# Up projection on the normalised x1 for three of its four quarters, first-norm sums in float32r, and another order in the last norm's tail

## Chip, core and metric

The kernel runs on one core of one Trainium2 chip. The metric is device time in microseconds (us). The kernel before takes 2334.99 us, the median of 3 runs (2334.02 to 2336.24). All matrix work is in 32-bit floats, most of it as float32r pairs.

## Reference

One layer of a hybrid decoder for 320 token columns (256 of a prompt, 8 x 8 of samples). Cut to what the change touches:

```python
merged = sigmoid(gate_a) * ya + sigmoid(gate_b) * yb
mix = merged @ w_out
x1  = LayerNorm(ALPHA * x + mix, ln1_g, ln1_b)          # ALPHA = 2 ** 0.25, D = 2048
hid = square(relu(x1 @ w_up))                           # 2048 -> 8192
ff  = hid @ w_down                                      # 8192 -> 2048
y   = LayerNorm(ALPHA * x1 + ff, ln2_g, ln2_b)
```

Before that stand one input projection, two recurrences (mLSTM and HGRN2) and two branch projections; the change leaves them as they are. The end states of the prompt, Cp and Sp, are outputs too, and are computed at the very end.

## The kernel before, in words

Activations lie transposed: 16 blocks of 128 channels (j or k, 0 to 15) by 320 token columns. A **tile** of the main stream is 128 output channels: 16 steps k, each of three matmuls in float32r, since weight and activation are each split in a rounded high part and a remainder: hi x hi, hi x lo, lo x hi (48 matmuls, accumulated in one bank of PSUM). The three are `self.mm(o, hi, mh)`, `self.mm(o, hi, ml)`, `self.mm(o, lo, mh)` in `run_main`; in the profile all matmuls have line L336. The tiles come in phases of 16: `wo` (w_out), then four quarters f = 0 to 3, each `up` (w_up) and `dn` (w_down). A phase is 768 matmuls. `moving(t)` says which activations a phase streams and which event each k waits for.

Weights arrive in units of 128 x 1024 (half a tile). `prep` splits each: ScalarE (ACT, L330, out `wh` or `bb`) writes the high part, VectorE (DVE, L475, out `wl` or `bb`) the remainder. Three buffers `wh`/`wl` serve from the start; at the start of `wo` the five wide buffers `wx` (in the memory `bb`) join them, so that eight units can be in flight. A unit's buffer is free again when PE has used it.

Everything else (evacuation of banks, the norms, the outputs) is written as generators that hand instructions to a list scheduler, `Sched`. It runs while the program is written: it keeps a clock per engine with fixed cost estimates and decides where in each engine's queue an instruction goes. On the chip every engine works through its queue in that order and waits by semaphores.

The first norm: `ev_wo` (L1790) makes z = ALPHA x + mix (L1797, L1801). After four tiles the sum S1 of z is added up over the channels by a matmul with a matrix of ones (`ln_add`, L1713), and the result c is taken off every z, so that later sums are small. S1 and S2 (sums of z and z squared, L1743, L1744) run on to j = 14; `ln_pre` multiplies them with ones and `ln_final` (L1754) adds the last z and its square by two more such matmuls: five in all, each in full float32. Then come mean M and 1/sigma RS by ACT and DVE (L1770 to L1778).

`up` doesn't wait for the norm: `zg` (L1814, L1819 in DVE's rows) splits z times gain into `xh`/`xl`, and two more columns there (320 and 321) carry the gain and the bias, so `up` streams 322 columns and `ev_up` (L1835) corrects the product with M and RS: `misc` from the two columns, L1840, L1842, ReLU, square, split into `ra`/`rxb` for `dn`. `x1` (L1822) makes ALPHA x1 for the residual, and `ev_dn` (L1852) adds each quarter of `dn` to it (L1857). In the last quarter the second norm's sums run along. **The tail** follows the last matmul of `dn`: ones matmuls, M and T (ACT), X (L1770, L1773, DVE), Ln and Exp (ACT), RS (L1776 to L1778, DVE), then per block subtract M (L1874) and multiply RS (L1879) on DVE in `y`, gain and bias on ACT and a DMA in `yb_`. Beside it `m_C` multiplies Cp (eight banks, copied out by ACT, `oC`) and `h_S` multiplies Sp (`oS`, four copies by ACT, four by DVE, L1557); SP issues all output DMAs in its queue's order.

Of the kernel before, what the change touches and what calls it, by code (L numbers as in the profile page):

```python
# [293 lines left out]
class Program:  # L294
# [251 lines left out]
    def moving(self, t):  # L546
        kind = t[0]
        if kind == "wa":
            return self.bah, self.bal, self.ba_ev
        if kind == "wb":  # L550
            return self.bbh, self.bbl, self.bb_ev
        if kind == "wo":
            return self.bah, self.bal, self.mg_ev
        if kind == "up":
            return self.xh2, self.xl2, self.zg_ev
        if kind == "dn":
            return self.bah, self.bal, self.hid_ev[t[2]]
        return self.xh, self.xl, None

    def before(self, i, t):  # L560
# [26 lines left out]
        elif kind == "wo" and h == 0:  # L587
# [3 lines left out]
            self.hl_free += [(s.t["pe"], x) for x in self.wx]  # L591
            s.spawn(self.ln_x(), 1)
        elif kind == "dn" and c == 3 and h == 0:
            self.carve_x()
        elif i == len(TILES) - 8:
            for j in range(MH):
                s.spawn(self.m_C(j), 3)
            for j in range(HH):
                s.spawn(self.h_S(j), 3)
# [477 lines left out]
    def m_C(self, h):  # L1077
# [7 lines left out]
        for c in range(2):  # L1085
# [8 lines left out]
            yield ("act", act(512, True), lambda: self.A(self.oC[h][:, c, :], b))  # L1094
# [603 lines left out]
    def ln_add(self, n, j, z, pre):  # L1698
# [4 lines left out]
        if j < 4:  # L1703
# [7 lines left out]
            if j == 3:  # L1711
                p = yield acq(self.sbank)
                yield ("pe", pe_f(TOK), lambda: self.mm(p[:, :TOK], self.ones, S1, start=True, stop=True))  # L1713
# [12 lines left out]
        if j == 15:  # L1726
            yield from self.ln_final(n, z)
            return
        yield from self.ln_sum(j, z)
        yield post(st["s"][j])  # L1730
        if j == 14:
            self.s.spawn(self.ln_pre(n), 0)

# [20 lines left out]
    def ln_final(self, n, z):  # L1754

        v = self.nc.vector
        st = self.ln[n]
        M, RS, X, T = (self.lnb[i] for i in (3, 4, 5, 6))
# [7 lines left out]
        yield post(st["fin"])  # L1766
        t = yield ("act", act(TOK, True), lambda: self.A(M, p1, scale=1.0 / D))
# [22 lines left out]
    def ev_wo(self, j, c, b):  # L1790
# [16 lines left out]
        if j == 15:  # L1807
            yield wait(*self.zg_ev)
            gb = self.vec[:, V_G1:V_G1 + 32]
            yield ("act", act(32), lambda: self.A(gb, gb, scale=ALPHA))  # L1810
# [21 lines left out]

    def ev_up(self, j, f, b):
        v = self.nc.vector

        sm = yield acq(self.sm)
# [13 lines left out]
    def ev_dn(self, j, f, b):  # L1850
# [6 lines left out]
        yield ("dve", dve(TOK, True), lambda: v.tensor_tensor(z, z, b[:, :TOK], ALU.add))  # L1857
# [8 lines left out]
    def y(self):  # L1866
# [4 lines left out]
        for i in range(KT + 2):  # L1871
# [3 lines left out]
            if i == 1:  # L1875
                yield wait(st["end"])
            if i > 1:
                z = self.acc[:, i - 2, :]
                t = yield ("dve", dve(TOK), lambda: v.tensor_tensor(z, z, self.lnb[4], ALU.mult), (0.0,))  # L1879
                self.s.spawn(self.yb_(i - 2, z), 0, t)  # L1880
# [9 lines left out]
    def run(self, pool):  # L1890
# [14 lines left out]
        self.acc_ev = [Ev() for _ in range(KT)]  # L1905
# [79 lines left out]
```

## Time and profile before

| | |
|---|---|
| median of 3 runs | 2334.99 us |
| the profiled execution's own time | 2335.47 us |
| its span, first to last instruction | 2333.5 us |
| PE busy | 2320.9 us (99%) |
| DVE busy, ACT busy | 1359.4 us (58%), 1074.2 us (46%) |
| granted TensorE clock | 0.998 |
| first matmul of `up` f = 0, f = 1, f = 2 | 1397.78, 1625.55, 1852.25 us |
| last matmul phase ends, first matmul of Cp | 2307.26 us |

Times inside the execution are us from the span's start. Matmuls overlap in a pipeline: one lasts some 310 ns in the record, but the next starts about 147 ns after it, so the distance between starts is what a matmul costs. A row of the timeline has start, duration, engine, line, operation, out<-in, shape and count, and in brackets how long the engine had been idle and what ended that; a row with x2 covers two instructions of one group. A float32 matmul (the ones) is recorded as x2.

### The profile page before, as it was taken

How to read it: one execution, taken by the hardware profiler on the slowest of the kernel's cores; microseconds unless marked ns; L12 is line 12 of the kernel's file. 1: busy time of each engine (PE TensorE's matmuls, PEld its weight loads, DVE VectorE, ACT ScalarE, POOL GpSimd, SP SyncE). 2: the span in 40 equal slices, each digit the busy share in tenths (PEclk: the TensorE clock that was granted, in tenths of full speed). 3: DMA queues.
4: the chain of work that ended last, by engine and by line, in shares of the span. 5: the costliest groups of instructions: out<-in, count | busy, mean ns of one | idle time of the engine just before them, and what ended most of it. 6: DMA issues, size and time to landing. Idle time of an engine off the chain costs nothing.

```text
span 2333.5 us, 38987 instructions
## 1 busy us (share of the span) xinstructions
PE 2320.9 (99%) x15812; PEld 2276.1 (98%) x15812; DVE 1359.4 (58%) x2304; ACT 1074.2 (46%) x1765; POOL 11.5 (0%) x36
## 2 busy tenths in 40 slices
PE   9999999999999999999999999999999999999998
PEld 8999999999999999999999999999999999999998
DVE  5565566667676776555555767544554455445555
ACT  4444445455566665444433546533443344334434
POOL 0000000000000000000000000000000000000000
PEclk9999999999999999999999999999999999999999
DMA  7576857665555555555555644444444444444465
GB/s 238 202 251 207 292 186 275 227 215 173 196 179 189 182 187 168 182 168 178 170 174 172 222 162 145 146 152 148 150 145 154 145 151 147 154 145 149 150 226 181
DMA packets 145627, 424.92 MB, mean 182 GB/s; under 512 B 18468, under 2 KB 39972, under 8 KB 144424
## 3 DMA queue, kind: packets, MB, share of 16 engines
q1 hardware_dynamic: 143864, 415.63, 53.6%
q0 software_dynamic: 1152, 6.29, 0.8%
q8 instruction: 123, 2.02, 0.3%
q10 hardware_dynamic: 432, 0.52, 0.1%
q14 instruction: 56, 0.46, 0.1%
HBM read 371.48 MB, written 50.90 MB: 181 GB/s over the span
## 4 chain that ended last, share of the span: by engine, by line
PE 97%; DMA 1%; DVE 1%; ACT 0%; issue 0%; SPq 0%; DVEq 0%; ACTq 0%
PE bank L336 95%; DMA wr<-wt 1%; DMA f<-xT 0%; DVE f3m L1874 0%; DVE f3m L1879 0%; PE bank L925 0%; PE bank L1586 0%; DMA gaD<-f 0%; PE bank L1151 0%; PE bank L1424 0%; DVE bb L475 0%; ACT wh L330 0%; ACT bb L330 0%; DVE wl L475 0%; ACT f L330 0%
## 5 line engine op out<-in xcount | busy, mean ns | idle before, releaser
L475 DVE TENSOR_TENSOR wl<-wr,wh 128x1024 fp32r<-128x1024 f32 x428 | 524.3, 1225 | 476.8 <-ACT wh L330 471.0
L336 PE MATMUL bank<-xh,wh 128*128 128x320 f32 (+1 forms) x2432 | 787.1, 324 | 2.2 <-ACT xh L330 2.2
L336 PE MATMUL bank<-xh,wl 128*128 128x320 f32 (+1 forms) x2432 | 754.9, 310 | 0.0
L336 PE MATMUL bank<-xl,wh 128*128 128x320 f32 (+1 forms) x2432 | 753.2, 310 | 1.3 <-DVE xl L681 1.3
L330 ACT ACTIVATE wh<-wr 128x1024 fp32r<-128x1024 f32 (+1 forms) x431 | 453.7, 1053 | 423.8 <-PE bank L336 403.3
L336 PEld LDWEIGHTS bank<-xh,wh 128*128 128x128 f32 x2432 | 459.5, 189 | 21.7 <-issue 15.5
L336 PEld LDWEIGHTS bank<-xl,wh 128*128 128x128 f32 x2432 | 460.0, 189 | 4.8 <-DVE xl L681 1.9
L336 PEld LDWEIGHTS bank<-xh,wl 128*128 128x128 f32 x2432 | 459.2, 189 | 0.0
L475 DVE TENSOR_TENSOR bb<-wr,bb 128x1024 fp32r<-128x1024 f32 x179 | 219.3, 1225 | 236.5 <-ACT bb L330 236.4
L336 PE MATMUL bank<-xh,bb 128*128 128x322 f32 x1280 | 287.2, 311 | 0.0
L330 ACT ACTIVATE bb<-wr 128x1024 fp32r<-128x1024 f32 x179 | 188.7, 1054 | 208.7 <-PE bank L336 197.7
L336 PE MATMUL bank<-ra,bb 128*128 128x320 f32 x1264 | 283.8, 309 | 0.0
L336 PE MATMUL bank<-rxb,bb 128*128 128x320 f32 x1112 | 255.4, 309 | 0.0
L336 PE MATMUL bank<-ra,wh 128*128 128x320 f32 x892 | 250.1, 309 | 0.0
L336 PEld LDWEIGHTS bank<-xh,bb 128*128 128x128 f32 x1280 | 215.9, 188 | 0.0
L336 PEld LDWEIGHTS bank<-ra,bb 128*128 128x128 f32 x1264 | 210.6, 188 | 0.4
L336 PE MATMUL bank<-xl,bb 128*128 128x322 f32 x640 | 198.7, 310 | 0.0
L336 PEld LDWEIGHTS bank<-rxb,bb 128*128 128x128 f32 x1112 | 188.4, 188 | 0.2
L330 ACT ACTIVATE f<-f,misc 128x320 f32<-128x320 f32 x210 | 118.1, 562 | 148.6 <-DVE f L1842 136.8
L336 PE MATMUL bank<-rxb,wh 128*128 128x320 f32 x596 | 184.4, 309 | 0.0
L336 PE MATMUL bank<-rxb,wl 128*128 128x320 f32 x596 | 183.9, 309 | 0.0
L336 PEld LDWEIGHTS bank<-ra,wh 128*128 128x128 f32 x892 | 161.4, 188 | 1.1 <-DVE ra L1616 1.0
(255 smaller groups left out, 2247.9 us busy)
## 6 DMA issues: line engine op xcount, KB each, us to landing
wr<-wt SPq DMA_DIRECT2D x607, 512.0 KB, 3.4
rx<-C SPq DMA_DIRECT2D x34, 256.0 KB, 5.3
Cs<-rx SPq DMA_DIRECT2D x34, 256.0 KB, 5.3
f<-C SPq DMA_DIRECT2D x30, 256.0 KB, 4.7
Cs<-f SPq DMA_DIRECT2D x30, 256.0 KB, 4.6
vD<-ra SPq DMA_DIRECT2D x4, 1024.0 KB, 7.2
f<-S SPq DMA_DIRECT2D x8, 512.0 KB, 6.0
f3h<-S SPq DMA_DIRECT2D x8, 512.0 KB, 6.3
```

Source lines behind the costliest of these rows:

```text
L330: return self.nc.scalar.activation(out, in_, func, **kw)
L336: self.nc.tensor.matmul(*a, **kw)
L475: self.V().tensor_tensor(lo, raw, hi.bitcast(F32), ALU.subtract)
```

## The change

It has four parts. (1) `up` f = 1 to 3 streams the finished x1, split into the same buffers `xh`/`xl` during `dn` f = 0 by the new `xs_` (16 times one ACT and one DVE instruction), 320 columns wide; its evacuation is only max(b, 0), square and split. f = 0 stays as it was. x1 is now kept without ALPHA, which `ev_dn` f = 0 applies (L1904 in the new file), after waiting for the split; the ACT instruction that scaled gain and bias goes. (2) The first norm's three sums (S1 after four blocks; S1 and S2 at the end, now with all 16 blocks in them) are split by `total` and multiplied with ones in float32r, two matmuls each. The split's memory is the fifth wide buffer, which joins the weight buffers only after the norm. (3) `y` subtracts M from six blocks, not two, before it waits for RS. (4) Two of the eight Cp copies go from ACT to DVE (L1099 in the new file).

How the queues change is shown at three places. First, DVE where `up` f = 0 ends and `dn` f = 0 begins. Before, a weight split, the two steps of the last `up` tile's evacuation (bank 85), a weight split, the split of that result into `ra`, and the first `dn` bank:

```order
L475 TENSOR_TENSOR bb<-wr,bb 128x1024
L1840 TENSOR_SCALAR f_76<-f_76,misc,bank_85 128x320
L1842 TENSOR_TENSOR f_76<-f_76 128x320
L475 TENSOR_TENSOR wl<-wr,wh 128x1024
L1616 TENSOR_TENSOR ra<-f_76,ra 128x320
L1857 TENSOR_TENSOR f3m<-f3m,bank_88 128x320
```

Now, with x1's remainders (out `xl`, by the same helper `split`, now L1623):

```order
L475 TENSOR_TENSOR bb<-wr,bb 128x1024
L1883 TENSOR_SCALAR f_76<-f_76,misc,bank_85 128x320
L1623 TENSOR_TENSOR xl<-f3m,xh 128x320
L1885 TENSOR_TENSOR f_76<-f_76 128x320
L475 TENSOR_TENSOR bb<-wr,bb 128x1024
L1623 TENSOR_TENSOR xl<-f3m,xh 128x320
L1623 TENSOR_TENSOR ra<-f_76,ra 128x320
L1623 TENSOR_TENSOR xl<-f3m,xh 128x320
L1904 TENSOR_SCALAR f3m<-f3m,bank_88 128x320
```

Two of the sixteen splits stand ahead of the split into `ra` that `dn` f = 0 needs at its last k; the other fourteen stand behind it.

Second, DVE around the first norm's sum over four blocks. Before, from the fourth z (bank 82) to the first subtraction of c:

```order
L1797 TENSOR_SCALAR f3m<-f_76,bank_82 128x320
L475 TENSOR_TENSOR bb<-wr,bb 128x1024
L1708 TENSOR_TENSOR f_76<-f_76,f3m 128x320
L475 TENSOR_TENSOR wl<-wr,wh 128x1024
L1719 TENSOR_TENSOR f3m<-f3m,f_76 128x320
```

Now the weight split behind the fourth z is one unit earlier in the weights' order (`wl`, where that was `bb`), and the split of S1 (out `bb`, from f_76) stands directly behind the last addition:

```order
L1826 TENSOR_SCALAR f3m<-f_76,bank_82 128x320
L475 TENSOR_TENSOR wl<-wr,wh 128x1024
L1715 TENSOR_TENSOR f_76<-f_76,f3m 128x320
L1623 TENSOR_TENSOR bb<-f_76,bb 128x320
L475 TENSOR_TENSOR wl<-wr,wh 128x1024
L1729 TENSOR_TENSOR f3m<-f3m,f_76 128x320
```

On PE the ones matmul stood behind 24 matmuls of the fifth `wo` tile; the two float32r ones now stand behind 30 and 36 of them. The last sums stood behind 30 and 36 matmuls of the sixteenth `wo` tile, and 27 and 33 of the first `up` tile; now the four stand behind 0, 6, 24 and 30 of the second `up` tile.

Third, DVE in the tail, from the last `dn` bank (81) on. Before:

```order
L1857 TENSOR_TENSOR f3m<-f3m,bank_81 128x320
L1874 TENSOR_TENSOR f3m<-f3m,f_76 128x320 x2
L1770 TENSOR_SCALAR f_76<-bank_87,f_76 128x320
L1773 TENSOR_SCALAR f_76<-f_76 128x320
L1776 TENSOR_SCALAR f_76<-f_76 128x320
L1777 TENSOR_TENSOR f_76<-f_76 128x320
L1778 TENSOR_SCALAR f_76<-f_76 128x320
L1874 TENSOR_TENSOR f3m<-f3m,f_76 128x320
L1879 TENSOR_TENSOR f3m<-f3m,f_76 128x320
```

Now:

```order
L1901 TENSOR_TENSOR f3m<-f3m,bank_81 128x320
L1099 COPY oC<-bank_84 128x512
L1921 TENSOR_TENSOR f3m<-f3m,f_76 128x320 x6
L1799 TENSOR_SCALAR f_76<-bank_87,f_76 128x320
L1802 TENSOR_SCALAR f_76<-f_76 128x320
L1805 TENSOR_SCALAR f_76<-f_76 128x320
L1099 COPY oC<-bank_88 128x512
L1806 TENSOR_TENSOR f_76<-f_76 128x320
L1807 TENSOR_SCALAR f_76<-f_76 128x320
L1921 TENSOR_TENSOR f3m<-f3m,f_76 128x320
L1926 TENSOR_TENSOR f3m<-f3m,f_76 128x320
```

All six subtractions stand ahead of X (L1799), none between X and RS; a Cp copy stands between two steps of RS.

The diff:

```diff
--- before.py
+++ after.py
@@ -552,7 +552,7 @@
         if kind == "wo":
             return self.bah, self.bal, self.mg_ev
         if kind == "up":
-            return self.xh2, self.xl2, self.zg_ev
+            return (self.xh, self.xl, self.xs_ev) if t[2] else (self.xh2, self.xl2, self.zg_ev)
         if kind == "dn":
             return self.bah, self.bal, self.hid_ev[t[2]]
         return self.xh, self.xl, None
@@ -588,10 +588,14 @@
             s.until(lambda: len(self.sbank.free) >= 5)
             self.mbank.free += self.sbank.free[:3]
             del self.sbank.free[:3]
-            self.hl_free += [(s.t["pe"], x) for x in self.wx]
+            self.hl_free += [(s.t["pe"], x) for x in self.wx[:4]]
+            R = self.Part(self.wxv[4].rearrange("p x s v -> p (x s v)"))
+            self.lns = [R.three(2, TOK) for _ in range(3)]
             s.spawn(self.ln_x(), 1)
         elif kind == "dn" and c == 3 and h == 0:
             self.carve_x()
+        elif kind == "dn" and c == 0 and h == 0:
+            s.spawn(self.xs_(), 0)
         elif i == len(TILES) - 8:
             for j in range(MH):
                 s.spawn(self.m_C(j), 3)
@@ -1091,7 +1095,10 @@
                 for n, (s, x, y) in enumerate((s, x, y) for s in range(2) for x, y in ((0, 0), (0, 1), (1, 0)))])
             if c == 1:
                 yield post(self.mh[h]["C"])
-            yield ("act", act(512, True), lambda: self.A(self.oC[h][:, c, :], b))
+            if h < 2 and c == 0:
+                yield ("dve", dve(512, True), lambda: self.nc.vector.tensor_copy(self.oC[h][:, c, :], b))
+            else:
+                yield ("act", act(512, True), lambda: self.A(self.oC[h][:, c, :], b))
             yield rel(self.mbank, b)
             yield ("sp", 620, lambda: self.dma(self.d["Cp"][h, :, c, :], self.oC[h][:, c, :]))
         yield rel(self.vx, w)
@@ -1710,7 +1717,10 @@
                 yield post(st["s"][j])
             if j == 3:
                 p = yield acq(self.sbank)
-                yield ("pe", pe_f(TOK), lambda: self.mm(p[:, :TOK], self.ones, S1, start=True, stop=True))
+                if n == 0:
+                    yield from self.total(p, S1, self.lns[0])
+                else:
+                    yield ("pe", pe_f(TOK), lambda: self.mm(p[:, :TOK], self.ones, S1, start=True, stop=True))
                 yield ("act", act(TOK, True), lambda: self.A(cb, p[:, :TOK], scale=1.0 / 512))
                 yield rel(self.sbank, p)
                 yield post(st["c"])
@@ -1723,13 +1733,26 @@
                 yield post(st["s"][3])
             return
         yield wait(st["s"][j - 1])
-        if j == 15:
+        if j == 15 and n == 1:
             yield from self.ln_final(n, z)
             return
         yield from self.ln_sum(j, z)
+        if j == 15:
+            p = self.ln[n]["p"] = yield acq(self.sbank, 2)
+            for i in range(2):
+                yield from self.total(p[i], self.lnb[i], self.lns[1 + i])
+            self.hl_free.append((self.s.t["pe"], self.wx[4]))
+            yield from self.ln_scale(n)
+            return
         yield post(st["s"][j])
-        if j == 14:
+        if j == 14 and n == 1:
             self.s.spawn(self.ln_pre(n), 0)
+
+    def total(self, p, x, hl):
+        hi, lo = hl[:, 0, :], hl[:, 1, :]
+        yield from self.split(x, hi, lo)
+        for i, y in enumerate((hi, lo)):
+            yield ("pe", 147, lambda: self.mm(p[:, :TOK], self.ones.bitcast(F32R), y, start=i == 0, stop=i == 1))
 
     def ln_sum(self, j, z):
         v = self.nc.vector
@@ -1753,9 +1776,7 @@
 
     def ln_final(self, n, z):
 
-        v = self.nc.vector
         st = self.ln[n]
-        M, RS, X, T = (self.lnb[i] for i in (3, 4, 5, 6))
         q = yield acq(self.tmp)
         t = yield ("act", act(TOK), lambda: self.A(q, z, AF.Square))
         yield wait(st["pre"])
@@ -1764,6 +1785,14 @@
         yield ("pe", pe_f(TOK), lambda: self.mm(p2, self.ones, q, start=False, stop=True))
         yield rel(self.tmp, q)
         yield post(st["fin"])
+        yield from self.ln_scale(n)
+
+    def ln_scale(self, n):
+
+        v = self.nc.vector
+        st = self.ln[n]
+        M, RS, X, T = (self.lnb[i] for i in (3, 4, 5, 6))
+        p1, p2 = (p[:, :TOK] for p in st["p"])
         t = yield ("act", act(TOK, True), lambda: self.A(M, p1, scale=1.0 / D))
         st["m"].t = t
         yield ("act", act(TOK, True), lambda: self.A(T, p1, AF.Square, scale=1.0 / D))
@@ -1806,8 +1835,6 @@
         yield from self.ln_add(0, j, z, j >= 4)
         if j == 15:
             yield wait(*self.zg_ev)
-            gb = self.vec[:, V_G1:V_G1 + 32]
-            yield ("act", act(32), lambda: self.A(gb, gb, scale=ALPHA))
             for i in range(KT):
                 yield from self.x1(i)
 
@@ -1830,9 +1857,25 @@
         yield post(self.acc_ev[j])
 
 
+    def xs_(self):
+
+        for j in range(KT):
+            yield wait(self.acc_ev[j])
+            yield from self.split(self.mm_[:, j, :], self.xh[:, j, :], self.xl[:, j, :])
+            yield post(self.xs_ev[j])
+
     def ev_up(self, j, f, b):
         v = self.nc.vector
 
+        if f:
+            q = yield acq(self.tmp)
+            yield ("dve", dve(TOK, True), lambda: v.tensor_scalar(q, b[:, :TOK], 0.0, None, ALU.max))
+            yield rel(self.mbank, b)
+            yield ("act", act(TOK), lambda: self.A(q, q, AF.Square))
+            yield from self.split(q, self.bah[:, j, :], self.bal[:, j, :])
+            yield rel(self.tmp, q)
+            yield post(self.hid_ev[f][j])
+            return
         sm = yield acq(self.sm)
         yield ("act", act(2, True), lambda: self.A(sm[:, 0:2], b[:, TOK:TOK + 2]))
         yield wait(self.ln[0]["end"])
@@ -1854,7 +1897,11 @@
         if f == 3 and j >= 4:
             yield wait(self.ln[1]["c"])
             yield ("dve", dve(TOK), lambda: v.tensor_tensor(z, z, self.lnb[2], ALU.subtract))
-        yield ("dve", dve(TOK, True), lambda: v.tensor_tensor(z, z, b[:, :TOK], ALU.add))
+        if f:
+            yield ("dve", dve(TOK, True), lambda: v.tensor_tensor(z, z, b[:, :TOK], ALU.add))
+        else:
+            yield wait(self.xs_ev[j])
+            yield ("dve", dve(TOK, True), lambda: v.scalar_tensor_tensor(z, z, ALPHA, b[:, :TOK], ALU.mult, ALU.add))
         yield rel(self.mbank, b)
         if f < 3:
             return
@@ -1868,16 +1915,16 @@
         v = self.nc.vector
         st = self.ln[1]
         yield wait(st["m"])
-        for i in range(KT + 2):
+        for i in range(KT + 6):
             if i < KT:
                 z = self.acc[:, i, :]
                 yield ("dve", dve(TOK), lambda: v.tensor_tensor(z, z, self.lnb[3], ALU.subtract), (0.0,))
-            if i == 1:
+            if i == 5:
                 yield wait(st["end"])
-            if i > 1:
-                z = self.acc[:, i - 2, :]
+            if i > 5:
+                z = self.acc[:, i - 6, :]
                 t = yield ("dve", dve(TOK), lambda: v.tensor_tensor(z, z, self.lnb[4], ALU.mult), (0.0,))
-                self.s.spawn(self.yb_(i - 2, z), 0, t)
+                self.s.spawn(self.yb_(i - 6, z), 0, t)
 
     def yb_(self, j, z):
         g, b = self.vec[:, V_G2 + j:V_G2 + j + 1], self.vec[:, V_B2 + j:V_B2 + j + 1]
@@ -1902,7 +1949,7 @@
         self.vD = [self.dr.tile([128, 2, 2, 512], F32, name=f"vD{j}") for j in range(MH)]
         self.ln = [dict(c=Ev(), end=Ev(), pre=Ev(), m=Ev(), fin=Ev(), s=[Ev() for _ in range(KT)]) for _ in range(2)]
         self.xq, self.xq_ev = [None] * KT, [Ev() for _ in range(KT)]
-        self.acc_ev = [Ev() for _ in range(KT)]
+        self.acc_ev, self.xs_ev = ([Ev() for _ in range(KT)] for _ in range(2))
         self.start()
         self.dma(n0, self.d["n0"])
         self.run_main()
```

## The prediction

> **What bounds the kernel now.** First the page: engines, and the chain that ended last, by engine.
>
> ```profile
> PE 2320.9 (99%) x15812; PEld 2276.1 (98%) x15812; DVE 1359.4 (58%) x2304; ACT 1074.2 (46%) x1765; POOL 11.5 (0%) x36
> ...
> PE 97%; DMA 1%; DVE 1%; ACT 0%; issue 0%; SPq 0%; DVEq 0%; ACTq 0%
> ```
>
> TensorE (PE) is the bound nearly everywhere. What leaves PE's stream shortens the time; what leaves DVE or ACT doesn't, except where PE waits for it, or in the tail. So I need what a matmul costs by width. Next, PE's timeline where `dn` f = 0, `up` f = 1, `dn` f = 1 and `up` f = 2 begin, with the one irregular place in `dn` f = 1.
>
> ```profile
> 1512.67 0.31 PE L336 MATMUL bank<-rxb,wh 128*128 128x320 f32 x1
> ...
> 1625.55 0.31 PE L336 MATMUL bank<-xh,wh 128*128 128x322 f32 x1
> ...
> 1739.37 0.31 PE L336 MATMUL bank<-rxb,wh 128*128 128x320 f32 x1
> ...
> 1745.97 0.70 PE L336 MATMUL bank<-ra,wh 128*128 128x320 f32 x2
> 1746.50 0.31 PE L336 MATMUL bank<-ra,wl 128*128 128x320 f32 x1
> ...
> 1852.25 0.31 PE L336 MATMUL bank<-xh,wh 128*128 128x322 f32 x1
> ```
>
> An `up` phase takes 1739.37 - 1625.55 = 113.82 us, 148.2 ns for each of 768 matmuls. A `dn` phase takes 112.88, of which about 0.24 is the place at 1745.97, where two matmuls take 0.53 instead of 0.29: there, at k = 15 of the first tile, PE waits for the last `up` tile's split. The rest is 112.64 us, 146.7 ns each. Is that the width, or the buffer `xh`? The projections ahead of `wo` stream 320 columns from it:
>
> ```profile
> 855.37 427.12 PE bank L336 x2912
> ```
>
> 427.12 / 2912 = 146.7 ns. So it is the width.
>
> **Part 1, narrower `up`.** Three phases fall from 113.82 to 112.64: **-3.54 us**. I know no cover for that; PE has no slack in these phases.
>
> The Trainium skill (TensorE: Matmul & The Clock Gate, "Back-to-back issue gap") gives N/2.4 + 2.5 ns for a warm matmul of N columns. By it two columns are worth 0.83 ns, an estimate: 1.9 us in all, and the forecast would stand at 2331.2. It would also give 135.8 ns for 320 columns; the trace has 146.7, so the trace decides.
>
> The evacuation of these 48 tiles loses one DVE and two ACT instructions a tile, all beside PE. It counts at one place only, the start of `dn`. DVE and ACT there, before (`up` f = 0 ended at 1512.67):
>
> ```profile
> 1515.16 0.54 DVE L1840 SCALAR_TENSOR_TENSOR f<-f,misc,bank 128x320 f32<-128x320 f32 x1
> 1515.74 0.49 DVE L1842 TENSOR_TENSOR f<-f 128x320 f32<-128x320 f32 x1
> ...
> 1519.01 0.48 DVE L1616 TENSOR_TENSOR ra<-f,ra 128x320 fp32r<-128x320 f32 x1
> ```
>
> ```profile
> 1516.79 1.04 ACT L330 ACTIVATE wh<-wr 128x1024 fp32r<-128x1024 f32 x1
> ...
> 1520.01 1.06 ACT L330 ACTIVATE wh<-wr 128x1024 fp32r<-128x1024 f32 x1 [1.30 <-PE bank L336]
> ```
>
> PE wants the remainder in `ra` 46 matmuls after 1512.67, at 1519.41; it is complete at 1519.49. Ahead of it, ACT's weight split at 1516.79 ran late, behind the ReLU that needs L1842. Without that ReLU (f = 1 to 3) it starts when PE frees its buffer, as the row at 1520.01 does; a unit (24 matmuls, 3.52) and its 0.24 wait before that is 1516.25. The remainder then comes 0.54 earlier, before it is wanted: three waits of 0.24 go, **-0.72**.
>
> In f = 0 the old evacuation stays, and two x1 splits get ahead of it. On DVE one step of 0.40 (the spacing of independent 128x320 steps, below) stands between L1840 and L1842, where a dependent step waited some 0.12 anyway; ReLU, weight split and its remainder move by about 0.22. The second stands directly before `ra`, 0.40 more. So `ra` comes 0.62 later, and that wait grows from 0.24 to 0.86: **+0.62** (bounds 0, no growth, and 1.3, two more splits ahead). The other fourteen lie beside PE, which has weights for six units in hand, and `up` f = 1 wants them 100 us later; without that cover each would cost its 0.40.
>
> **Part 2, first norm.** PE at the start of `wo`, at its first and second ones matmul, and at the start of `up` f = 0:
>
> ```profile
> 1282.45 0.31 PE L336 MATMUL bank<-rxb,wh 128*128 128x320 f32 x1
> ...
> 1313.99 0.30 PE L336 MATMUL bank<-rxb,wl 128*128 128x320 f32 x1
> 1315.10 0.81 PE L336 MATMUL bank<-f,ones 128*128 128x320 f32 x2 [0.81 <-DVE f L1708]
> ...
> 1315.89 0.31 PE L336 MATMUL bank<-ra,wh 128*128 128x320 f32 x1
> ...
> 1394.07 0.70 PE L336 MATMUL bank<-f,ones 128*128 128x320 f32 x2
> ...
> 1394.75 0.31 PE L336 MATMUL bank<-ra,bb 128*128 128x320 f32 x1
> ...
> 1397.78 0.31 PE L336 MATMUL bank<-xh,wh 128*128 128x322 f32 x1
> ```
>
> From 1394.07 to 1394.75 lie one ones matmul and one ordinary one: 0.68 - 0.147 = 0.53 us. Five go (2.67), six in float32r come. HGRN2 has such ones matmuls in float32r already; the groups of PE, shapes apart:
>
> ```profile
> L336 PE MATMUL bank<-ra,ones 128*128 128x320 f32 x16 | 5.0, 314 | 0.0
> ```
>
> One lasts 314 ns in the record, like an ordinary matmul (0.31 above), so I give it an ordinary one's 0.147: 0.88, and **-1.79** in all.
>
> The first ones matmul comes 1.11 us after its predecessor, and the next-but-one 0.79 after it: against 0.147 and 0.68 that is a stall of 1.07. DVE shows why:
>
> ```profile
> 1313.42 1.22 DVE L475 TENSOR_TENSOR bb<-wr,bb 128x1024 fp32r<-128x1024 f32 x1 [1.36 <-ACT bb L330]
> 1314.57 0.48 DVE L1708 TENSOR_TENSOR f<-f,f3m 128x320 f32<-128x320 f32 x1
> ```
>
> The last addition stands behind a weight split that waits for its weights. In the new queue the unit ahead of it is one earlier. That unit reuses a buffer of three that PE frees at the eighth unit's end, 1282.45 + 8 x 3.52 = 1310.6; ACT 1.06 and DVE 1.14 more, then the addition ends about 1313.4, S1's parts stand at 1313.9 and 1314.4. PE comes to them 30 and 37 matmuls into the fifth tile, at 1315.0 and 1316.0. So the stall goes: **-1.07**; bound 0, if weights come late.
>
> The norm's end moves too. DVE there, before: `zg`'s remainder of block 15, and RS:
>
> ```profile
> 1403.69 0.55 DVE L1819 SCALAR_TENSOR_TENSOR xl<-f3m,vec,xh 128x320 fp32r<-128x320 f32 x1
> ...
> 1409.51 0.49 DVE L1778 SCALAR_TENSOR_TENSOR f<-f 128x320 f32<-128x320 f32 x1
> ```
>
> The remainder was complete at 1404.24, 6.5 us after `up` began. A step of S1's split now stands directly ahead of it (0.40), so 6.9, and PE wants it after 46 matmuls, 6.8, no longer put off by ones matmuls in this tile: **+0.15** (0 to 0.5). RS was complete 12.2 us after `up` began; its steps now each stand behind weight splits that come one in 3.56 us, and counted through the queue it comes at about 24.6. That costs nothing while six banks last: the seventh `up` tile begins at 6 x 7.11 = 42.7.
>
> **Parts 3 and 4, the tail.** DVE, ACT and SP at its decisive places:
>
> ```profile
> 2309.87 0.89 DVE L1874 TENSOR_TENSOR f3m<-f3m,f 128x320 f32<-128x320 f32 x2 [1.91 <-ACT f L330]
> 2310.68 0.48 DVE L1770 SCALAR_TENSOR_TENSOR f<-bank,f 128x320 f32<-128x320 f32 x1
> ...
> 2312.90 0.49 DVE L1776 SCALAR_TENSOR_TENSOR f<-f 128x320 f32<-128x320 f32 x1 [1.38 <-ACT f L330]
> ...
> 2314.37 0.48 DVE L1874 TENSOR_TENSOR f3m<-f3m,f 128x320 f32<-128x320 f32 x1
> ...
> 2326.43 1.41 DVE L1557 COPY oS<-bank 128x256 f32<-128x256 f32 x4
> ```
>
> ```profile
> 2311.55 0.47 ACT L330 ACTIVATE f<-f 128x320 f32<-128x320 f32 x1 [1.39 <-DVE f L1773]
> 2311.93 0.58 ACT L330 ACTIVATE oC<-bank 128x512 f32<-128x512 f32 x1
> 2312.41 0.46 ACT L330 ACTIVATE f<-f 128x320 f32<-128x320 f32 x1
> ...
> 2315.29 0.66 ACT L330 ACTIVATE f3m<-f3m,vec 128x320 f32<-128x320 f32 x1 [0.62 <-DVE f3m L1879]
> ...
> 2324.43 3.05 ACT L330 ACTIVATE f3m<-f3m,vec 128x320 f32<-128x320 f32 x5
> ```
>
> ```profile
> 2327.32 1.02 SPq L339 DMA_DIRECT2D y<-f3m  x2
> 2328.43 0.95 SPq L339 DMA_DIRECT2D Sp<-oS  x2
> ```
>
> DVE starts one independent step each 0.40 us (30 from 2314.37 to 2326.43), and had 1.38 idle while ACT made Ln and Exp. But the four added subtractions stand ahead of X: it starts 4 x 0.40 = 1.61 later, and the idle time stays, shorter by 0.36 because no copy stands between Ln and Exp (0.86 apart, where Ln alone lasts 0.47 and hands over in 0.03). The copy between L1805 and L1806 lengthens RS again. A 128x256 copy takes 0.33 (four in 1.41), so 128x512 lies between 0.33 and 0.66; I take 0.60, less the 0.13 that a dependent step waits anyway: 0.47. RS and the next subtraction come 1.61 - 0.36 + 0.47 = 1.7 later, at 2316.1, with 26 steps left, not 30: DVE ends its blocks at 2326.5 instead of 2326.43. DVE gains nothing.
>
> The Trainium skill (VectorE: DVE Perf Modes, "The TRN2 errata") prices a copy out of PSUM at 120 + N cycles of 0.96 GHz, 0.66 us for 512 as an estimate; by it the sum would be 0.06 worse.
>
> ACT is the one that counts: from 2315.29 to 2327.48 it worked without pause (16 blocks, 4 Cp and 4 Sp copies), and SP's last four issues follow its last blocks. It now starts 1.7 later with one copy (0.48 from start to start) less, and ends 1.2 to 1.3 later. Of SP's two issues from 2327.32 the second, for ACT's last block, began about 0.3 behind that block's end, so SP's last issue moves by **+1.0** (bounds: 0 if DVE's order mattered alone, 1.9 with the dearest copy and no slack).
>
> **Sum**: -3.54 - 0.72 + 0.62 - 1.79 - 1.07 + 0.15 + 1.0 = -5.35. The profiled execution's own time is 2335.47 (span 2333.5), 0.48 above the median, so 2330.1 in its terms and **2329.6** as a median.
>
> **Rivals.**
> (A) The narrower stream brings nothing, because 148.2 ns is not width but the busier DVE and ACT beside `up`. For it: `dn` has less beside it. Against it:
>
> ```profile
> 860.00:945.00 85.00, 85.00 (x583) 85.00 (x582) 55.63 (x80) 47.12 (x70) 0.00 (x0) 1.00 0.53 173
> 1410.00:1510.00 100.00, 100.00 (x677) 100.00 (x677) 66.27 (x104) 58.78 (x103) 0.00 (x0) 1.00 0.46 149
> ```
>
> The columns are window, length, then busy time of PE, weight load, DVE, ACT: DVE is busy 65% of the first stretch (320 columns) and 66% of the second (322). Time: 2329.6 + 3.54 = 2333.1; chance 0.07.
> (B) The tail does what the added subtractions are for: they fill the 1.38 idle, and ACT starts no later. Then ends move by -1.0 at most, since PE's own tail and four Sp copies hold the rest: 2327.6. Against it: the queue's order. Chance 0.10.
> (C) The stall at the first sum stays, since the split waits for the late weights as the addition did: 2330.7, chance 0.20. For it: the weights' DMA is what DVE's queue waits for in this stretch.
> (D) Slower: RS comes so late that six `up` tiles fill the six banks and PE stops in `up` f = 0. This decides from 42.7 us after `up` began, each us beyond costs one, and from 48.0 on the whole 5.35 is gone; at 50 the time is 2334.99 + 2.0 = 2337.0. For it: RS doubles its distance. Against it: 24.6 leaves 18 in hand. Chance 0.03.
>
> **How the numbers follow.** The forecast has 0.60. Low end 2326.8: case B without the 0.62 and 0.15 of waits. High end 2332.8: case C with the upper bounds of `dn`'s wait (+0.7), `up`'s start (+0.4) and the tail (+0.9, and 0.1 rounding); A and D lie outside. A measurement of this kernel can tell about 0.2%, 4.7 us, from no change, so faster means below 2330.3. The forecast lies 0.7 below that, with steps of some 1 us uncertain: 0.42 of its 0.60 count as faster, 0.18 as the same. B counts as faster (0.10), C 0.08 to 0.12, A as the same, D as slower. That is 0.60, 0.37, 0.03.
>
> **What would show it.** Right: `up` f = 1 to 3 at 112.6 us each; no gap at 1315 and six float32r ones matmuls 0.15 apart from their successors; `dn` f = 0 about 0.6 longer, f = 1 and 2 0.24 shorter; the first Cp matmul 6.35 earlier, but ACT's last block only 5.1 and SP's last issue only 5.35 earlier. Wrong: a PE wait in the early tiles of `up` f = 0, `up` phases at 113.8, or ACT's first block in the tail no later, counted from the first Cp matmul.

## The result, and the profile after

| | before | after |
|---|---|---|
| median of 13 runs each, us | 2334.99 (2332.79 to 2336.94) | 2330.05 (2327.19 to 2332.39) |
| ratio, 95% interval | | 0.998 (0.9972 to 0.9987) |
| profiled execution's own time, span, us | 2335.47, 2333.5 | 2327.19, 2325.1 |

The interval makes 3.0 to 6.5 us of gain; the medians are 4.94 apart, the forecast was 5.35. The two profiled spans lie 8.4 apart, and that is more than the change does: 2.65 of it is there already when `wo` begins (1282.45 before, 1279.80 after), where both programs run the same instructions in the same order. So I count from the first matmul of `wo`.

First the page of the changed kernel: engines, and the chain that ended last by engine.

```profile
PE 2312.7 (99%) x15808; PEld 2270.0 (98%) x15808; DVE 1346.9 (58%) x2279; ACT 1055.1 (45%) x1685; POOL 11.5 (0%) x36
...
PE 98%; ACT 1%; DMA 1%; SPq 0%; DVE 0%; issue 0%; ACTq 0%; DVEq 0%
```

PE still bounds it. In the chain that ended last, DVE's 1% is gone and ACT has 1%: the end of the tail hangs on ACT. Next, PE's timeline, the first matmul of `wo`, `up` f = 0, `dn` f = 0, `up` f = 1, `dn` f = 1, `up` f = 2, and of Cp, with the place in `dn` f = 0 where PE waits.

```profile
1279.80 0.31 PE L336 MATMUL bank<-rxb,wh 128*128 128x320 f32 x1
...
1392.73 0.31 PE L336 MATMUL bank<-xh,bb 128*128 128x322 f32 x1
...
1507.36 0.31 PE L336 MATMUL bank<-rxb,bb 128*128 128x320 f32 x1
...
1513.66 0.60 PE L336 MATMUL bank<-ra,bb 128*128 128x320 f32 x3
1514.92 0.56 PE L336 MATMUL bank<-ra,bb 128*128 128x320 f32 x2 [0.66 <-DVE ra L1623]
...
1620.92 0.31 PE L336 MATMUL bank<-xh,bb 128*128 128x320 f32 x1
...
1733.37 0.31 PE L336 MATMUL bank<-rxb,bb 128*128 128x320 f32 x1
...
1846.01 0.31 PE L336 MATMUL bank<-xh,bb 128*128 128x320 f32 x1
...
2297.81 0.39 PE L336 MATMUL bank<-bb,wh 128*128 128x512 f32 x1
```

Each difference of starts is a phase:

| phase | before, us | after, us | change | forecast |
|---|---|---|---|---|
| `wo` | 115.33 | 112.93 | -2.40 | -2.38 |
| `up` f = 0 | 114.89 | 114.63 | -0.26 | -0.33 |
| `dn` f = 0 | 112.88 | 113.56 | +0.68 | +0.62 |
| `up` f = 1, 2, 3, each | 113.82 | 112.45 | -1.37 | -1.18 |
| `dn` f = 1, 2, 3, each | 112.88, 112.88, 114.49 | 112.64, 112.64, 114.25 | -0.24 | -0.24 |
| Cp's first matmul to the span's end | 26.25 | 27.28 | +1.03 | +1.0 |
| from `wo` to the end | | | -5.8 | -5.35 |

PE's one large wait from `wo` on is in `dn` f = 0: the third matmul of the row at 1513.66 starts at 1513.96, and the next one 0.96 behind it instead of 0.147. The one after that loses 0.1 more, so PE waits 0.92 in all. DVE's split of `ra` is named. DVE there:

```profile
1512.84 1.23 DVE L475 TENSOR_TENSOR bb<-wr,bb 128x1024 fp32r<-128x1024 f32 x1 [1.64 <-ACT bb L330]
1513.98 0.48 DVE L1623 TENSOR_TENSOR xl<-f3m,xh 128x320 fp32r<-128x320 f32 x1
1514.38 0.48 DVE L1623 TENSOR_TENSOR ra<-f,ra 128x320 fp32r<-128x320 f32 x1
```

The middle row is a split of x1 that nobody wants for another 100 us, directly ahead of the one that PE waits for. DVE at the first sum in `wo`:

```profile
1309.11 1.23 DVE L475 TENSOR_TENSOR wl<-wr,wh 128x1024 fp32r<-128x1024 f32 x1 [0.46 <-ACT wh L330]
1310.25 0.48 DVE L1715 TENSOR_TENSOR f<-f,f3m 128x320 f32<-128x320 f32 x1
```

The weight split ahead of the last addition starts 29.31 us after `wo` (1309.11 - 1279.80); before the change it started 30.97 after it (1313.42 - 1282.45). The addition comes 1.67 earlier, and PE has no gap there any more. Last, the tail of the changed kernel: DVE, then ACT, then SP's last two issues.

```profile
2300.41 2.50 DVE L1921 TENSOR_TENSOR f3m<-f3m,f 128x320 f32<-128x320 f32 x6 [0.32 <-ACT f L330]
2302.82 0.48 DVE L1799 SCALAR_TENSOR_TENSOR f<-bank,f 128x320 f32<-128x320 f32 x1
...
2304.71 0.49 DVE L1805 SCALAR_TENSOR_TENSOR f<-f 128x320 f32<-128x320 f32 x1 [1.04 <-ACT f L330]
2305.12 0.68 DVE L1099 COPY oC<-bank 128x512 f32<-128x512 f32 x1
2305.72 0.48 DVE L1806 TENSOR_TENSOR f<-f 128x320 f32<-128x320 f32 x1
```

```profile
2303.70 0.97 ACT L330 ACTIVATE f<-f 128x320 f32<-128x320 f32 x2 [1.24 <-DVE f L1802]
...
2307.57 1.46 ACT L330 ACTIVATE f3m<-f3m,vec 128x320 f32<-128x320 f32 x2 [1.00 <-DVE f3m L1926]
...
2316.45 2.83 ACT L330 ACTIVATE f3m<-f3m,vec 128x320 f32<-128x320 f32 x5
```

```profile
2320.01 0.96 SPq L339 DMA_DIRECT2D Sp<-oS  x2
```

Six subtractions stand ahead of X, DVE still idles 1.04 us behind it, and ACT's first block starts 9.76 us after Cp's first matmul (8.03 before). ACT's last block ends at 2319.28, and SP's last issue follows at 2320.5.

### The profile page after: what moved, and what is told of

It reads as the page before. It is cut to its first block, busy times and chain, and to the rows that moved or that the text cites. A ratio compares the mean times of both kernels' runs of the same rounds, so it can differ in the third digit from the quotient of the medians.

```text
span 2325.1 us, 38931 instructions
## 1 busy us (share of the span) xinstructions
PE 2312.7 (99%) x15808; PEld 2270.0 (98%) x15808; DVE 1346.9 (58%) x2279; ACT 1055.1 (45%) x1685; POOL 11.5 (0%) x36
## 4 chain that ended last, share of the span: by engine, by line
PE 98%; ACT 1%; DMA 1%; SPq 0%; DVE 0%; issue 0%; ACTq 0%; DVEq 0%
PE bank L336 96%; DMA wr<-wt 1%; SPq L339 0%; ACT f3m L330 0%; PE bank L1158 0%; PE bank L929 0%; PE bank L1593 0%; PE bank L1431 0%; DVE f3m L1921 0%; ACT f L330 0%; PE bank L1485 0%; PE bank L1436 0%; PE bank L1002 0%; PE bank L976 0%; PE bank L1542 0%
## 5 line engine op out<-in xcount | busy, mean ns | idle before, releaser
L336 PE MATMUL bank<-xh,bb 128*128 128x320 f32 (+1 forms) x1280 | 285.4, 309 | 0.0
L336 PE MATMUL bank<-rxb,bb 128*128 128x320 f32 x1208 | 276.3, 309 | 0.0
L336 PE MATMUL bank<-ra,wh 128*128 128x320 f32 x988 | 265.9, 309 | 0.0
L336 PE MATMUL bank<-ra,bb 128*128 128x320 f32 x1096 | 264.3, 309 | 0.7 <-DVE ra L1623 0.7
L336 PEld LDWEIGHTS bank<-rxb,bb 128*128 128x128 f32 x1208 | 204.5, 188 | 0.2
L336 PE MATMUL bank<-xl,bb 128*128 128x320 f32 (+1 forms) x640 | 197.7, 309 | 0.0
L336 PEld LDWEIGHTS bank<-ra,bb 128*128 128x128 f32 x1096 | 187.1, 188 | 1.2 <-DVE ra L1623 0.9
L336 PEld LDWEIGHTS bank<-ra,wh 128*128 128x128 f32 x988 | 176.3, 188 | 0.0
L336 PE MATMUL bank<-rxb,wh 128*128 128x320 f32 x548 | 169.0, 308 | 0.0
L336 PEld LDWEIGHTS bank<-xl,bb 128*128 128x128 f32 x640 | 120.4, 188 | 0.3 <-DVE xl L1846 0.3
```

The lines of the kernel that those rows point to most:

```text
L336: self.nc.tensor.matmul(*a, **kw)
```

## The experiments

Each run below is a single execution with its profile, but for the last, which has seven. Single executions of one kernel scatter by 2 us and more, so effects near 1 us are read from phases and from distances to Cp's first matmul. The same phase repeats to 0.1 us: `wo` took 112.92 or 112.93 in every kernel that has the change's first norm.

**The width of `up`.** Two thirds of the forecast's gain (3.54 of 5.35) rest on two columns. This run gives the changed kernel its 322 columns back and leaves the new, shorter evacuation:

```diff
-            return (self.xh, self.xl, self.xs_ev) if t[2] else (self.xh2, self.xl2, self.zg_ev)
+            return (self.xh2, self.xl2, self.xs_ev) if t[2] else (self.xh2, self.xl2, self.zg_ev)
```

> The changed kernel, in which the up projection's second to fourth quarters stream 322 columns again, out of the same buffers (the last two columns' products are not used). Theory (each column streamed costs PE time, and nothing else in these phases does): 148.2 ns a matmul and 113.8 us a phase, as before the change, against 146.4 ns and 112.45. Rival A (the shorter evacuation on DVE and ACT made the pace): 146.4 ns, 112.45 us. A mixture, 1.5 ns for the width and 0.3 for the evacuation: 147.9 ns, 113.6 us. Other phases as in the changed kernel.

PE's timeline of this run, first matmul of `up` f = 1 and of `dn` f = 1:

```profile
1620.85 0.31 PE L336 MATMUL bank<-xh,bb 128*128 128x322 f32 x1
...
1734.67 0.31 PE L336 MATMUL bank<-rxb,bb 128*128 128x320 f32 x1
```

113.82 us, 148.2 ns a matmul, as before the change to the last digit. `dn` stayed at 112.64. The two columns make the difference; the evacuation's part is nothing that can be seen. Rival A falls.

But 1.76 ns for two columns is dear: by that price 320 columns would take 282 ns. So the price of a column was measured at other widths, by the same edit with other slices (318, 312 and 256 leave tokens out of the product). For 328 each matmul reads on into the neighbouring block, and both buffers, `xh` and `xl`, are made six columns longer, which moves what lies behind them in memory.

> The changed kernel, in which the up projection's second to fourth quarters stream 318 columns: two tokens are left out of this product, so their results are not those of the reference. It measures the price of a column below 320. Theory (a price by column, from 322 to 320: 1.78 ns for two): 144.7 ns a matmul, 111.1 us a phase, 1.3 less than at 320. Rival 1 (322 pays for an odd size, not for two columns): 146.4 ns, 112.45 us. Rival 2 (about half a nanosecond a column, and the rest of the 1.78 was the evacuation): 145.6 ns, 111.8 us.

> As the run with 256 columns, with 312: 8 tokens are left out of this product. Theory (floor): 145.5 to 146.1 ns, 111.8 to 112.2 us a phase. Rival 1 (0.14 ns a column): 145.3 ns, 111.6 us. Rival 2 (0.9 ns a column below 318): 140.8 ns, 108.1 us.

> The changed kernel, in which the up projection's second to fourth quarters stream 256 columns; 64 tokens are left out of this product, so their results are not those of the reference. 322, 320 and 318 columns gave 148.19, 146.43 and 146.15 ns a matmul: two columns are worth 1.76 ns above 320 and 0.28 below. Theory (below 320 something else than the columns sets the pace, such as the weight load that comes with each matmul, so there is a floor): 145 to 146 ns, 111.4 to 112.2 us a phase. Rival 1 (0.14 ns a column all the way down): 137.4 ns, 105.5 us. Rival 2 (0.9 ns a column from somewhere below 318): under 100 ns, under 77 us.

> The changed kernel, in which the up projection's second to fourth quarters stream 328 columns (the last eight are neighbours in the buffer, and their products are not used). Theory (above 320 each column has its price, 0.88 ns as from 320 to 322): 153.5 ns, 117.9 us a phase. Rival 1 (one step between 320 and 322, then 0.14 ns a column as below): 149.0 ns, 114.5 us. Rival 2 (about half of it, 0.4 ns a column beyond the step): 150.6 ns, 115.7 us.

The same two rows of PE in the runs with 256 columns, with 318, and with 328:

```profile
1623.26 0.28 PE L336 MATMUL bank<-xh,bb 128*128 128x256 f32 x1
...
1714.55 0.32 PE L336 MATMUL bank<-rxb,bb 128*128 128x320 f32 x1
```

```profile
1623.14 0.31 PE L336 MATMUL bank<-xh,bb 128*128 128x318 f32 x1
...
1735.36 0.31 PE L336 MATMUL bank<-rxb,bb 128*128 128x320 f32 x1
```

```profile
1628.80 0.31 PE L348 MATMUL bank<-xh,bb 128*128 128x328 f32 x1
...
1744.86 0.31 PE L348 MATMUL bank<-rxb,bb 128*128 128x320 f32 x1
```

| columns | 256 | 312 | 318 | 320 | 322 | 328 |
|---|---|---|---|---|---|---|
| `up` f = 1, us | 91.29 | 110.68 | 112.22 | 112.45 | 113.82 | 116.06 |
| ns a matmul (divided by 768) | 118.9 | 144.1 | 146.1 | 146.4 | 148.2 | 151.1 |
| ns a column from the width to the left | | 0.45 | 0.33 | 0.15 | 0.89 | 0.49 |

The theories on record for these four fall; the nearest was rival 2 at 328 columns (115.7 us, measured 116.06). There is no floor: 256 columns run at 118.9 ns, not 145. There is no uniform 0.88 or 0.14 either. From 256 to 328 a column costs 0.45 ns on average ((151.1 - 118.9) / 72), with bends: 320 lies about 1.1 ns below the straight line from 256 to 328 (147.5 there), 322 about 0.2 below it (148.4). So of the 1.76 ns that two columns brought here, 0.9 is the average price and 0.9 is the bend at 320.

The bend is not a property of the width alone. A phase's mean hides that the 16 blocks k of one buffer run at paces of their own. In the changed kernel's second tile of `up` f = 1, the first matmuls of blocks 9, 10 and 11:

```profile
1631.91 0.31 PE L336 MATMUL bank<-xh,wh 128*128 128x320 f32 x1
...
1632.36 0.31 PE L336 MATMUL bank<-xh,wh 128*128 128x320 f32 x1
...
1632.80 0.31 PE L336 MATMUL bank<-xh,wh 128*128 128x320 f32 x1
```

The three matmuls of block 9 take 0.45, those of block 10 take 0.44. From the unrounded starts, as the mean over the 16 tiles of `up` f = 1, in ns a matmul, for some blocks:

| block | 2 | 3 | 4 | 6 | 9 | 15 | all 16 |
|---|---|---|---|---|---|---|---|
| 320 columns (changed kernel) | 148.2 | 145.0 | 147.8 | 143.9 | 150.3 | 144.7 | 146.4 |
| 322 columns (first run above) | 146.7 | 150.9 | 146.1 | 148.1 | 148.9 | 151.1 | 148.2 |

f = 2 and f = 3 give the same to 0.1 ns, so this is no scatter. Two more columns made block 15 dearer by 6.4 ns and blocks 2, 4, 9 and 12 cheaper, by 0.8 to 1.7. In `dn` all blocks take 146.6 to 146.7; they lie 320 columns apart in memory, those of `xh` and `xl` 322 apart. And at one and the same width the place counts: in the run with 328 columns the projections ahead of `wo` stream 320 columns as ever, but their tiles that read `xh` and `xl` took 147.8 ns a matmul, where all eleven other programs have 146.9. So the gain from 322 to 320 is real for these buffers, while the bends of the table are sums over 16 places, and the entry for 328 has a shift of place in it. Which property of a place decides stays open.

**The wait at `dn` f = 0.** The x1 splits start one tile later:

```diff
-        elif kind == "dn" and c == 0 and h == 0:
+        elif kind == "dn" and c == 0 and h == 1:
             s.spawn(self.xs_(), 0)
```

> The changed kernel, in which the sixteen splits of x1 start one tile later in the first down phase. Theory (two of these splits stand ahead of the last up tile's split on DVE and ACT, and PE waits for that at the 46th matmul): the wait falls from 0.92 us to the 0.24 of before, down f = 0 from 113.56 to 112.88 us, and nothing waits later, since the second up quarter wants the splits 100 us on. Rival (the wait grew because the weights' split or the old evacuation of this quarter is later in the new order, not for the x1 splits): 113.5, no change.

PE in this run, first matmul of `dn` f = 0 and of `up` f = 1; then DVE where `ra` is split:

```profile
1508.76 0.31 PE L336 MATMUL bank<-rxb,bb 128*128 128x320 f32 x1
...
1621.64 0.31 PE L336 MATMUL bank<-xh,bb 128*128 128x320 f32 x1
```

```profile
1513.96 1.23 DVE L475 TENSOR_TENSOR bb<-wr,bb 128x1024 fp32r<-128x1024 f32 x1 [1.64 <-ACT bb L330]
1515.10 0.49 DVE L1623 TENSOR_TENSOR ra<-f,ra 128x320 fp32r<-128x320 f32 x1
```

112.88 us, and `ra` directly behind the weight split: the two x1 splits made the whole 0.68. The later phases are unchanged (112.42, 112.64, 112.45), so the splits have time to spare.

**The stall at the first sum.** The kernel before, with one weight buffer fewer until the norm is done, its sums and their places untouched:

```diff
-            self.hl_free += [(s.t["pe"], x) for x in self.wx]
+            self.hl_free += [(s.t["pe"], x) for x in self.wx[:4]]
...
         yield post(st["fin"])
+        if n == 0:
+            self.hl_free.append((self.s.t["pe"], self.wx[4]))
```

> The kernel before, with one edit: of the five wide weight buffers that join at wo, four join there and the fifth at the end of the first norm's sums. The sums stay in float32, once for three and twice for thirteen blocks, and stand where they stood. Theory (with one buffer fewer, one weight unit fewer is split ahead, so the last addition no longer stands behind a split that waits for weights): no stall at the first ones matmul, wo 115.33 - 1.07 = 114.26 us. Rival (the stall went because the sum is split first and its ones matmuls come later in the stream): the stall stays at about 1.1 us, wo at 115.3. Everything from up on as before the change.

PE in this run: first matmul of `wo`, then the first ones matmul with its neighbours, then the first of `up` f = 0; and DVE ahead of that sum:

```profile
1282.54 0.31 PE L336 MATMUL bank<-rxb,wh 128*128 128x320 f32 x1
...
1314.07 0.31 PE L336 MATMUL bank<-rxb,wl 128*128 128x320 f32 x1
1314.22 0.70 PE L336 MATMUL bank<-f,ones 128*128 128x320 f32 x2
1314.51 0.55 PE L336 MATMUL bank<-rxb,wh 128*128 128x320 f32 x1
...
1396.79 0.31 PE L336 MATMUL bank<-xh,bb 128*128 128x322 f32 x1
```

```profile
1311.85 1.23 DVE L475 TENSOR_TENSOR wl<-wr,wh 128x1024 fp32r<-128x1024 f32 x1 [0.46 <-ACT wh L330]
1312.99 0.48 DVE L1708 TENSOR_TENSOR f<-f,f3m 128x320 f32<-128x320 f32 x1
```

The ones matmul follows its predecessor at 0.15; before, at 1.11. `wo` takes 114.25, 1.08 less: the stall goes by the buffer count alone. The place of the sums, the rival on record for this run, has no part in it, and rival C of the forecast falls too. The weight split ahead of the addition starts 29.31 after `wo` here, exactly as in the changed kernel. What is left between this run's 114.25 and the changed kernel's 112.93 is 1.32 for the float32r sums; three float32 ones matmuls against two float32r were forecast at 3 x 0.535 - 2 x 0.147 = 1.31. The run's own time was 2334.62, within the scatter of before; only the phase shows it.

**The tail: order or copies?** Two runs, one edit each on the changed kernel. First the subtractions two ahead again:

```diff
-        for i in range(KT + 6):
+        for i in range(KT + 2):
...
-            if i == 5:
+            if i == 1:
...
-            if i > 5:
-                z = self.acc[:, i - 6, :]
+            if i > 1:
+                z = self.acc[:, i - 2, :]
```

> The changed kernel with the last norm's subtractions two ahead again, as before the change; the copies of Cp stay as the change has them (two on DVE). The order that the scheduler then writes also puts one Cp copy back between Ln and Exp on ACT. Theory (four subtractions stand ahead of X in DVE's queue, 0.40 us each, and ACT's unbroken work starts that much later): X 1.6 us earlier, Ln to Exp 0.86 apart and no longer 0.50, so ACT's first block starts 8.5 us behind the first Cp matmul (9.76 in the changed kernel), its last block ends at 20.2 (21.47), and the span ends 26.0 behind the first Cp matmul (27.28). Rival (the Cp copies that moved to DVE lengthen the tail): first block at 9.8, span end at 27.3, no change. Phases ahead of the tail as in the changed kernel.

DVE and ACT in this run; its Cp began at 2300.35 and its span ended 26.00 later:

```profile
2303.76 0.48 DVE L1799 SCALAR_TENSOR_TENSOR f<-bank,f 128x320 f32<-128x320 f32 x1
...
2305.98 0.49 DVE L1805 SCALAR_TENSOR_TENSOR f<-f 128x320 f32<-128x320 f32 x1 [1.38 <-ACT f L330]
```

```profile
2304.63 0.47 ACT L330 ACTIVATE f<-f 128x320 f32<-128x320 f32 x1 [1.39 <-DVE f L1802]
2305.01 0.58 ACT L330 ACTIVATE oC<-bank 128x512 f32<-128x512 f32 x1
2305.49 0.46 ACT L330 ACTIVATE f<-f 128x320 f32<-128x320 f32 x1
...
2309.00 1.30 ACT L330 ACTIVATE f3m<-f3m,vec 128x320 f32<-128x320 f32 x2
...
2317.18 3.86 ACT L330 ACTIVATE f3m<-f3m,vec 128x320 f32<-128x320 f32 x6
```

X starts 3.41 after Cp's first matmul (5.01 in the changed kernel), the first block 8.65 (9.76), and the tail is 1.28 shorter. The edit isn't quite pure: in the order that the scheduler then writes, a Cp copy stands between Ln and Exp again. And one expected figure was missed: ACT's last block ended at 20.69, not at 20.2. Its last six blocks took 3.86, where five took 2.83 in the changed kernel, since they now wait for DVE, which needs two steps of 0.40 a block (two of the six start 0.04 behind the end of DVE's step). That the span still ended at the expected 26.0 is in part luck: SP had two issues to make behind that block's end here (y, Sp), three in the changed kernel (y, Sp, Sp). Second, all Cp copies on ACT again, subtractions still six ahead:

```diff
-            if h < 2 and c == 0:
-                yield ("dve", dve(512, True), lambda: self.nc.vector.tensor_copy(self.oC[h][:, c, :], b))
-            else:
-                yield ("act", act(512, True), lambda: self.A(self.oC[h][:, c, :], b))
+            yield ("act", act(512, True), lambda: self.A(self.oC[h][:, c, :], b))
```

> The changed kernel with all Cp copies on ACT again; the last norm's subtractions stay six ahead. Theory (the order of the subtractions is what made the tail longer): X no earlier; a copy between Ln and Exp on ACT again (+0.36) and none between L1805 and L1806 on DVE (-0.47), so ACT's first block starts at 9.6 to 9.8 us behind the first Cp matmul (9.76), with one copy more to do (+0.48): last block's end at 21.5 to 22.0 (21.47), span end 27.3 to 27.8 (27.28). Rival (the copies on DVE made it longer): span end back at 26.3, as before the change.

ACT's first block in this run, and SP's last three issues; Cp began at 2302.04, the span ended 27.61 later:

```profile
2311.66 0.66 ACT L330 ACTIVATE f3m<-f3m,vec 128x320 f32<-128x320 f32 x1 [1.44 <-DVE f3m L1923]
```

```profile
2323.82 1.62 SPq L339 DMA_DIRECT2D Sp<-oS  x3
```

The first block at 9.62 instead of 9.76, the tail 0.33 longer. ACT's last block ended at 21.32, a little before the expected 21.5 to 22.0, but an Sp copy follows it on ACT, and three Sp issues on SP. So with six subtractions ahead the copies on DVE are worth 0.33, and with two ahead 0.25 (26.25 before, 26.00 in the first of these runs). The four more subtractions ahead cost 1.28 with copies on DVE, 1.36 without (27.61 - 26.25).

**A better version.** The narrow `up` and the new sums stay; the splits come one tile later; four subtractions run ahead, two of them behind the step after X, where DVE idles; one Cp copy stays on DVE, and the Cp copy next in line on ACT waits until Exp is done (`x` is set behind L1802's step, `exp` behind Exp):

```diff
-        elif kind == "dn" and c == 0 and h == 0:
+        elif kind == "dn" and c == 0 and h == 1:
...
+                if h == 0:
+                    yield wait(self.ln[1]["exp"])
-            if h < 2 and c == 0:
+            if h == 0 and c == 0:
...
-        for i in range(KT + 6):
+        for i in range(KT + 4):
+            if i == 2:
+                yield wait(st["x"])
...
```

> The changed kernel with three edits: the x1 splits one tile later; the last norm's subtractions four ahead, of which two stand ahead of X and two behind the step after it, where DVE has about 1 us idle; and of the two Cp copies on DVE the second back on ACT, where the Cp copy next in line waits until Exp is done. Theory: down f = 0 at 112.9 (0.7 less); X 1.6 us earlier, Ln to Exp still 0.50 apart, no copy among the steps of RS (0.47 less): ACT's first block 7.7 us behind the first Cp matmul (9.76), one copy more on ACT than in the changed kernel (+0.48), span end 25.7 (27.28). In all 2.3 us below the changed kernel, 2327.7, 0.997 of the time before. Rival (ACT or SP hold the tail by their own work, from M on, whatever DVE's order is): span end no earlier than 26.8, and 0.7 to 1.2 in all.

DVE, then ACT and SP; Cp began at 2299.39:

```profile
2303.55 0.89 DVE L1927 TENSOR_TENSOR f3m<-f3m,f 128x320 f32<-128x320 f32 x2
2304.68 0.49 DVE L1809 SCALAR_TENSOR_TENSOR f<-f 128x320 f32<-128x320 f32 x1 [0.24 <-ACT f L330]
```

```profile
2307.06 0.66 ACT L330 ACTIVATE f3m<-f3m,vec 128x320 f32<-128x320 f32 x1 [0.28 <-DVE f3m L1932]
```

```profile
2320.25 0.95 SPq L339 DMA_DIRECT2D Sp<-oS  x2
```

DVE's idle time behind X shrank from 1.04 to 0.24, two subtractions in it. The first block starts 7.67 after Cp's first matmul, as expected; the span ended at 25.95, 0.25 later than expected, since SP's last issues moved by 1.34 where ACT's last block moved by 1.58. `dn` f = 0 took 112.89. By phases that is 0.67 + 1.33 = 2.0 less than the changed kernel. The median of 7 runs was 2327.98 against 2335.09 (11 runs of before): ratio 0.9968, interval 0.9957 to 0.9979. This interval overlaps the changed kernel's, so the totals alone would not tell the two apart; the phases do.

## Why the prediction was right, step by step

- **Narrower `up`**: the mechanism right, the size too small: -4.11 for -3.54. The forecast took 146.7 ns, the pace of `dn`, for 320 columns; `up` itself runs at 146.4, and `dn` stayed at 146.7 in every run. The forecast's step "so it is the width", and not the buffer, doesn't hold: of the 2912 matmuls that it divides by, 1376 read `xh` or `xl`, and tiles that read only those took 146.9. The buffer counts too, block by block, as the runs above show; that the mean over its blocks at 320 came out near 146.7 was partly luck. The Trainium skill (TensorE: Matmul & The Clock Gate, "Back-to-back issue gap") would have had 0.83 ns for two columns, an estimate by its formula for the gap of an isolated matmul. The 0.417 ns a column in it is near the runs' mean of 0.45, but its level is not (109.2 ns for 256 columns, an estimate too; 118.9 here), and it doesn't give the bend at 320, for which the neighbouring phase was the better guide.
- **The waits at `dn`**: -0.72 at f = 1 to 3, as forecast. At f = 0 the wait grew by 0.68 (forecast 0.62), for the reason given: the run with later splits took all of it back. Of the 0.68, 0.40 is the split directly ahead of `ra`; the part that comes through ACT was 0.28, not 0.22.
- **Float32r sums**: -1.31 forecast for the three in `wo`, 1.32 measured between two kernels that differ there by nothing else on PE. All six new ones matmuls stand 0.14 to 0.15 from their successors. `up` f = 0 got 0.26 instead of 0.33: PE waits 0.25 us for `xl` of block 15 where 0.15 was allowed.
- **The stall**: -1.07 forecast, -1.08 by the buffer count alone.
- **The end of the norm**: RS was complete 22.0 us after `up` began (L1807's start 1414.23 plus 0.49, less 1392.73), where 24.6 was counted. No bank ran out, and rival D had 20 us to go.
- **The tail**: +1.03 for +1.0; six ahead alone costs 1.36, and the moved copies give 0.33 back. ACT's first block came 1.73 later (1.7 forecast) and its last 1.25 later (1.2 to 1.3). Rival B falls: DVE idled 1.38 before and 1.04 after, because the added work stood ahead of X and not behind it. The copy of 128 x 512 on DVE took 0.60 from its start to the next one's (2305.12 to 2305.72), the value taken between 0.33 and 0.66.
- **The sum**: -5.8 by phases, -4.94 between the medians, -5.35 forecast. The 0.57 that `up` gave beyond its term is more than the difference from the phases' sum, and small misses the other way make up the rest. The median's distance lies inside its interval, so the 0.8 between phases and medians needs no cause. That the median came within 0.5 of the forecast's 2329.6 is therefore partly luck; the phases are the better witness. The forecast drew its line for "faster" at 2330.3: the median is 0.25 below it, but the interval (2328.5 to 2332.0) reaches over it, so the totals don't decide that.

## What to carry to other kernels

When PE bounds a kernel, price an edit by phases, not by the total: here phases repeat to 0.1 us while totals scatter by 2, and a change of 1 us is plain in the one and invisible in the other. Work put ahead of a dependent chain in a queue doesn't fill that chain's idle time, it delays the chain; to fill it, it has to stand behind the step that starts the wait (four more subtractions ahead of X cost 1.28 us; two behind it fitted into DVE's idle time, with 0.24 of it left). A background job whose result is wanted much later should start one step after a phase boundary, where the short queue to the next phase's first operands is.

## What was not expected of the hardware

- Matmuls of one shape don't run at one pace: with 320 columns out of `xh` and `xl` the blocks of one tile take from 143.9 to 150.3 ns a matmul, the same in every tile to 0.3 ns, while those of `dn` all take 146.6 to 146.7. Where the blocks lie counts, at one width by up to 0.8 ns in the mean (146.9 and 147.8). So a price by column, 0.45 ns on average from 256 to 328, is uneven in the small: two columns beyond 320 cost 1.37 us here in a phase of 768 matmuls.
- Ahead of `wo`, with the same instructions in the same order, `wo` began at 1279.80 in the changed kernel's profile, at 1282.45 in that of before and at 1284.04 in the run with all copies on ACT. PE's delays up to there (starts more than 0.45 us apart, less 0.147 each) came to 6.7, 8.3 and 10.1 us. So a good part of this scatter is waits of PE early on that differ from one execution to the next. The part that differs lies in the first 30 us, where the profile puts most of them down to the splits of weights and of the input (into `xh` and `xl`), and at 370 us (up to 1.2 us, behind an ACT result); what makes these late wasn't followed up. The scatter is nearly as large as the change's effect.
